# Moving the weight sums of a down-projection beside the up-projection, with its first left factors loaded and split early

## The chip, the cores and the metric

The kernel runs on one core of one Trainium2 chip. The metric is the device time of one execution in microseconds (us), as the median of three runs. The core has five engines that work at the same time, each through its own list of instructions in order: TensorE (PE, with its weight loads PEld), VectorE (DVE), ScalarE (ACT), GpSimd (POOL) and SyncE (SP). All DMA transfers of this kernel are issued by SP, in the order of its list.

## The reference, cut to what matters

One step of a decoder layer: a mixing block (an mLSTM beside a convolution module), cross-attention into 256 memory tokens, and a ConvFFN, for 2048 prompt tokens and 64 sample tokens. The change lies in the ConvFFN and at its entry.

```python
# D_MODEL = 1024, D_FF = 2816, SEQ = 2048, 8 sample rows of 8 tokens
hf = rmsnorm(x, w['norm_ffn'])
uf = hf @ w['f_wup']
fa, fg = uf[..., :D_FF], uf[..., D_FF:]
f_ext = jnp.concatenate([f_buf.astype(fa.dtype), fa], axis=1)
fa_c = causal_dwconv(f_ext, w['f_conv_w'], w['f_conv_b'])      # width 3
x = x + (jax.nn.gelu(fa_c) * fg) @ w['f_wdown']
...
y_prompt = rmsnorm(xp, norm_final)
```

All of it is float32, and the result must be that of float32 products.

## The kernel before, in words

**Products.** A float32 product is made of three matmuls: each operand is split into a high part (rounded to the matmul's type by a ScalarE cast) and a low part (the rest, a subtraction on VectorE or GpSimd), and `mm3` (L153) adds high x high, high x low and low x high. `split` (L295) makes the two parts. Large products are cut into two by two quarters and made of seven products instead of eight (`seven_products`, L1058): of each operand there are three quarters (B11, B21, B22) and four sums (T1 to T4), the "factors". `left_sums` (L1050) makes the four sums of one operand.

**Up-projection.** The prompt is taken in three blocks of 6, 5 and 5 row tiles of 128 tokens (`C_BLOCKS`); the last also has the sample tokens. `rows_in` loads and norms the rows of a block (six buffers `xt` in the pool `xw`), in two halves z; `block_input` transposes them and makes the seven right factors R. T1 and T4 are made on GpSimd. Then eleven steps p follow, each with two `load_pair` calls (for the value columns a and the gate columns g): raw weights come in, and seven split weights `wt` (a ring of ten tiles) go to `seven_products`. In block 0 the four sums of each weight pair are made and stored; blocks 1 and 2 load them. VectorE adds the products, convolves, and multiplies with the gate; the result's left factors for the down-projection go to DRAM (`l_d`).

**Down-projection.** For each of the seven products q (order B11, B21, T2, T3, T1, B22, T4) the eleven right factors are loaded and split (`right_factors_down`); for each of eight row tiles j a left factor `lr` (128 x 11 x 128) is loaded and split into `l`, and 33 matmuls of 512 columns follow. One (q, j) is called a unit here; there are 56, counted from 0. The row tiles `acc` (`x2_d`, the residual) are loaded beside the first two products: eight for B11, eight for B21. `weight_sums` runs beside units 1 to 11: it loads two 128-row slices of `f_wdown`, multiplies the sample rows with them (`psG`), makes the four sums on VectorE and GpSimd, and stores them (`ds`) for the products T2, T3, T1 and T4.

**What sets the order.** The code is written as a sequence; a scheduler then puts each engine's instructions in order, by the code's order and by when it reckons that operands and tiles are free, so that work can stand far from where the code has it. Tiles come from pools with a fixed number of buffers; a pool opened in the place of a closed one waits, tile by tile, for what lay in its memory. Pools with `side="right"` grow from the other end.

Of the kernel before, what the change touches and what calls it, by code (L numbers as in the profile page):

```python
# [19 lines left out]
P = 128  # L20
D = 1024
# [70 lines left out]
R_ORDER = 1, 2, 3, 0, 4, 5, 6  # L92
# [4 lines left out]
def trunk_kernel(ctx: ExitStack, tc: tile.TileContext, i: dict, o: list):  # L97
# [1341 lines left out]
    def rows_in(blk, junk=None):  # L1439

        t0, nt_, smp = blk
        hc = nt_ * P // 2
        halves = []
        for z in range(2):
            xts = []
            first, n = t0 * P + z * hc, hc + (HS if smp else 0)
            for c0 in range(0, n, P):
                nt = min(P, n - c0)
                t = xw.tile([P, D], F32, name="xt", tag="xt")
                c = c0  # L1450
                while c < c0 + nt:
                    if c < hc:
                        tid, r0 = divmod(first + c, P)
                        m = min(P - r0, c0 + nt - c, hc - c)
                    else:
                        tid, r0, m = NT, z * HS, HS
                    SY.dma_start(t[c - c0:c - c0 + m], x2_d[tid][r0:r0 + m])
                    c += m
                norm_x([(t, nt)], junk() if junk else fe_.tile([P, D], BF16, name="junk", tag="junk"), V)
                xts.append((t, nt))  # L1460
            halves.append(xts)
        return halves
# [158 lines left out]
    def factors():  # L1621
        return [wfp.tile([P, 2, KT // 2, 512], F32R, name=f"wf{q}", tag=f"wf{q}") for q in range(7)]
# [37 lines left out]
    ahead = rows_in(C_BLOCKS[0], junk_rows)  # L1660
# [5 lines left out]
    wtp = ctx.enter_context(tc.tile_pool(name="wtf", bufs=WT_BUFS, side="right", reuse_waits="tile"))  # L1666
    f2 = us.enter_context(tc.tile_pool(name="f2", bufs=2, side="right", reuse_waits="tile"))
# [10 lines left out]
    def block_input(blk, rows):  # L1678

        n = width(blk)  # L1680
        R = {}

        def btile():
            return fe_.tile([P, HM], F32, name="b", tag="b", bufs=KT)[:, :n]

        def feature(xts, k):
            pt = tps()
            c = 0
            for t, nt in xts:
# [9 lines left out]
        b11, t3 = [btile() for _ in half], [utile(n) for _ in half]  # L1699
        for q in R_ORDER:  # L1700
# [48 lines left out]
    def raw_tile():  # L1749
        return f2.tile([P, 2, 512], F32, name="raw", tag="raw", bufs=RAW_BUFS)  # L1750
# [54 lines left out]
    R_next = block_input(C_BLOCKS[0], ahead)  # L1805
    for bi, (t0, nt_, smp) in enumerate(C_BLOCKS):
# [6 lines left out]
        for p in range(FP):  # L1813
# [77 lines left out]
    lp = ctx.enter_context(tc.tile_pool(name="lp", bufs=2, side="right", reuse_waits="tile"))  # L1891
# [35 lines left out]

    sums_d = [[dram(f"ds{kh}_{k}", [P, 2, 512]) for k in range(FP)] for kh in range(2)]
# [4 lines left out]
    def weight_sums(k):  # L1933

        r = []
        for kh in range(2):
            t = xw.tile([P, 2, 512], F32, name="wr", tag="xt")
            SY.dma_start(t, wdn[(2 * k + kh) * P:(2 * k + kh + 1) * P, :].rearrange("p (c d) -> p c d", c=2))
            for c in range(2):
                mm(pts[c * S:(c + 1) * S], ysr[:, 2 * k + kh], t[:, c], k + kh == 0, k + kh == FP)  # L1940
            r.append(t)
        (b11, b12), (b21, b22) = [[t[:, c] for c in range(2)] for t in r]
        tt(b22, b22, b12, ALU.subtract)
        tt(b12, b12, b11, ALU.subtract, G)
# [22 lines left out]
    def left_factor(q, j):  # L1967
        raw = lp.tile([P, FP, P], F32, name="lr", tag="lr")
        r = 0
        for b, c, m in segments(j):  # L1970
            SY.dma_start(raw[:, :, r:r + m], l_d[b][q, :, :, c:c + m])
            r += m
        w = lp.tile([P, 2, FP, P], F32R, name="l", tag="l")
        split(w[:, 0], w[:, 1], raw)
        return w
# [9 lines left out]

    accs = [], []
    for qi, q in enumerate((B11, B21, T2, T3, T1, B22, T4)):
# [3 lines left out]
        for j in range(NJ):  # L1991
            l = left_factor(q, j)
            if qi < 2:
                accs[qi].append(acc_rows(qi, j))
            pt = dps()
            for k in range(FP):
                mm3(pt, (l[:, 0, k], l[:, 1, k]), (ws[k][:, 0], ws[k][:, 1]), k == 0, k == FP - 1)
            c = cs[j]
            x00, x01, x10, x11 = [accs[z][j][:, c_ * 512:(c_ + 1) * 512] if z <= qi else None
# [29 lines left out]
            if qi < 2 and 0 < qi * NJ + j <= FP:  # L2029
                weight_sums(qi * NJ + j - 1)  # L2030
# [3 lines left out]
        elif q == B21:  # L2034
# [37 lines left out]
```

## Time and profile before

| | us |
|---|---|
| runs | 2940.2, 2941.53, 2950.7 |
| median | 2941.53 |
| profiled execution | 2940.78 |
| its span | 2939.1 |
| TensorE busy | 2733.7 (93%) |
| VectorE busy | 2053.4 (70%) |
| ScalarE busy | 1395.5 (47%) |
| GpSimd busy | 1204.5 (41%) |

The span runs from the first to the last recorded instruction; 1.7 us lie around it. The ConvFFN takes the second half: the first matmul with R starts at 1466.5, the up-projection's last ends at 2450.8, the down-projection's last at 2931. A share over the whole span says little here, since the stages have different limits; the views by stage, below, are read with the time of each stage in mind. [...]

### The profile page before, as it was taken

Reading aid. Unit: us, or ns where it says so; the run is one execution under the profiler, and the core shown is the slowest. Engines: PE = TensorE matmul, PEld = TensorE weight load, DVE = VectorE, ACT = ScalarE, POOL = GpSimd, SP = SyncE. Lnnn points to the kernel's source line nnn. Section 1 sums busy time; section 2 is a strip of 40 time slices with the busy share of each in tenths; the row PEclk is TensorE's granted clock in tenths of the full one; section 3 lists DMA queues with packets and bytes.
Section 4 is the critical chain, followed back from the end, with each engine's and each line's share of the span. In section 5 each row is a group of like instructions: output and inputs, shape, how many; then the busy total and the mean of one; then the engine's idle time right before and its main releaser. Section 6 shows DMA issues by size and latency. Waiting matters only on the chain. (4 is left out here: it accounts for less than half of the span.)

```text
span 2939.1 us, 44186 instructions
## 1 busy us (share of the span) xinstructions
PE 2733.7 (93%) x15768; PEld 2409.4 (82%) x15768; DVE 2053.4 (70%) x3393; ACT 1395.5 (47%) x2777; POOL 1204.5 (41%) x1287
## 2 busy tenths in 40 slices
PE   7999999989799799899799999999999997899998
PEld 6889899966577778676589899899989996578887
DVE  4588898783224788755389999888898885354454
ACT  4576678871223665512364334644454452232233
POOL 1458565460220533534365444554464442113200
PEclk9999999998899999999899999999999998999999
DMA  7635433344557423757644555566656557994454
GB/s 184 196 123 181 125 91 120 90 155 140 180 171 238 159 69 100 241 177 248 215 157 164 178 182 167 173 205 197 198 173 187 174 178 225 307 290 137 138 167 131
DMA packets 428532, 509.37 MB, mean 173 GB/s; under 512 B 61613, under 2 KB 331667, under 8 KB 428304
## 3 DMA queue, kind: packets, MB, share of 16 engines
q1 hardware_dynamic: 428312, 506.55, 54.5%
q8 instruction: 124, 2.03, 0.3%
q14 instruction: 96, 0.79, 0.1%
HBM read 346.67 MB, written 160.15 MB: 172 GB/s over the span
## 5 line engine op out<-in xcount | busy, mean ns | idle before, releaser
L297 ACT CAST wt<-raw 128x512 fp32r<-128x512 f32 x542 | 325.6, 618 | 366.4 <-DVE raw L128 66.7
L128 DVE TENSOR_TENSOR wt<-raw,wt 128x512 fp32r<-128x512 f32 x374 | 337.5, 907 | 89.2 <-ACT wt L297 88.7
L128 POOL TENSOR_TENSOR wt<-raw,wt 128x512 fp32r<-128x512 f32 x168 | 251.5, 1498 | 192.3 <-ACT wt L297 171.6
L128 POOL TENSOR_TENSOR cside<-cside,cprod 128x512 f32<-128x512 f32 (+2 forms) x248 | 251.4, 1014 | 120.7 <-ACT cprod L120 82.3
L125 DVE SCALAR_TENSOR_TENSOR psG<-ue,vc,psG 128x512 f32<-128x512 f32 (+2 forms) x448 | 256.7, 573 | 22.8 <-ACT psG L120 15.2
L151 PE MATMUL psA<-R,wt 128*128 128x384 f32 (+2 forms) x1392 | 246.4, 328 | 6.0 <-DVE u L128 2.5
L151 PEld LDWEIGHTS psA<-R,wt 128*128 128x128 f32 x1392 | 229.3, 191 | 8.3 <-ACT wt L297 3.1
L297 ACT CAST l<-lr 128x1408 fp32r<-128x1408 f32 x56 | 77.1, 1376 | 284.2 <-PE psA L151 68.7
L120 ACT ACTIVATE cprod<-ue,vc 128x512 f32<-128x512 f32 (+2 forms) x248 | 146.8, 605 | 30.0 <-POOL cside L128 22.2
L151 PE MATMUL psA<-wf,l 128*128 128x512 f32 x516 | 133.0, 406 | 10.0 <-DVE u L128 5.8
L125 DVE SCALAR_TENSOR_TENSOR y<-fe,vc,y 128x640 f32<-128x640 f32 (+1 forms) x132 | 137.2, 1073 | 6.5 <-ACT y L120 6.5
L128 DVE TENSOR_TENSOR l<-lr,l 128x1408 fp32r<-128x1408 f32 x56 | 98.9, 1766 | 60.1 <-ACT l L297 57.5
L151 PE MATMUL psG<-R,wt 128*128 128x320 f32 (+2 forms) x696 | 128.7, 327 | 4.9 <-DVE fe L128 2.4
L151 PE MATMUL psE<-R,wt 128*128 128x352 f32 (+2 forms) x696 | 127.4, 326 | 5.7 <-DVE u L128 3.1
L151 PE MATMUL psD<-R,wt 128*128 128x320 f32 (+2 forms) x696 | 127.0, 326 | 5.5 <-DVE u L128 3.3
L151 PE MATMUL psC<-R,wt 128*128 128x384 f32 (+2 forms) x684 | 124.4, 328 | 7.8 <-DVE u L128 7.2
L144 POOL TENSOR_TENSOR r<-v,nhalf 128x1 f32<-128x1 f32 (+1 forms) x63 | 39.9, 634 | 222.6 <-DVE v L134 221.3
L151 PE MATMUL psF<-R,wt 128*128 128x352 f32 (+2 forms) x696 | 126.5, 325 | 3.2 <-DVE fe L128 2.5
L151 PEld LDWEIGHTS psA<-wf,l 128*128 128x128 f32 x516 | 97.6, 194 | 38.6 <-issue 13.2
L128 POOL TENSOR_TENSOR y<-y,u 128x384 f32<-128x384 f32 (+2 forms) x66 | 78.4, 1188 | 122.8 <-ACT wt L297 53.1
L151 PE MATMUL psB<-R,wt 128*128 128x384 f32 (+2 forms) x684 | 123.8, 326 | 1.3 <-DVE R L128 0.7
L151 PE MATMUL psD<-h,wt 128*128 128x256 f32 (+1 forms) x768 | 116.7, 297 | 7.5 <-DMA h<-h 4.8
(663 smaller groups left out, 6927.0 us busy)
## 6 DMA issues: line engine op xcount, KB each, us to landing
raw<-in_f_wup SPq DMA_DIRECT2D x88, 512.0 KB
raw<-sum SPq DMA_DIRECT2D x88, 512.0 KB
lr<-l SPq DMA_DIRECT2D x49, 704.0 KB
sum<-raw SPq DMA_DIRECT2D x44, 512.0 KB
xt<-x SPq DMA_DIRECT2D x42, 512.0 KB
xt<-in_x_prompt SPq DMA_DIRECT2D x32, 512.0 KB
x<-xt SPq DMA_DIRECT2D x32, 512.0 KB
h<-h SPq DMA_DIRECT2D x56, 256.0 KB
```

The source lines that it names most:

```text
L120: A.activation(out, in_, func, bias=bias, scale=scale)
L125: V.scalar_tensor_tensor(out=out, in0=in0, scalar=s, in1=in1, op0=op0, op1=op1)
L128: (eng or V).tensor_tensor(out=out, in0=a, in1=b, op=op)
L144: G.tensor_tensor(out=y, in0=v, in1=e.to_broadcast(sh), op=ALU.pow)
L151: T.matmul(out, lhsT, rhs, start=start, stop=stop)
L297: A.copy(hi, src)
```

## The change

- `weight_sums` is called in the up-projection, at the steps listed in `SUMS_AT` (block 1, p = 0 to 6, and block 2, p = 1 to 4); all four sums are on GpSimd, and it no longer multiplies the sample rows.
- `sample_rows` multiplies the sample rows with one 128-row slice of `f_wdown`, beside units 1 to 22; `f_wdown` is loaded for it once more (`ws`).
- The left factors are loaded two units ahead in the code (`left_raw`), the first two into buffers of `xw` shared with other tiles ("common"), with high priority; the first is split into three weight tiles (`left_first`). The buffers of `lr` lie in the pool `dp`, and `l` has two named tiles.
- The second eight `acc` tiles are loaded at the third product T2 in the code, not the second.
- `rows_in` takes one half z; of block 0, the second half is loaded and normed inside `block_input`, after the factors B11 and B21.
- The order in which pools and tiles are laid out changes: `wf` reversed, raw weights in a pool of their own, R in another order, the convolution's carries behind R.

```diff
-R_ORDER = 1, 2, 3, 0, 4, 5, 6
+SUMS_AT = [(1, p) for p in range(7)] + [(2, p) for p in range(1, 5)]
+ACC_AT = 0, 2
+R_ORDER = 1, 2, 3, 4, 0, 5, 6
...
-    def rows_in(blk, junk=None):
+    def rows_in(blk, z, junk=None):
...
-        return [wfp.tile([P, 2, KT // 2, 512], F32R, name=f"wf{q}", tag=f"wf{q}") for q in range(7)]
+        return [wfp.tile([P, 2, KT // 2, 512], F32R, name=f"wf{q}", tag=f"wf{q}") for q in range(6, -1, -1)][::-1]
...
-    ahead = rows_in(C_BLOCKS[0], junk_rows)
+    ahead = rows_in(C_BLOCKS[0], 0, junk_rows)
...
+    rawf = us.enter_context(tc.tile_pool(name="rawf", bufs=RAW_BUFS, side="right", reuse_waits="tile"))
...
-        xts, xts1 = rows
+        xts = rows[0]
...
+        xts1 = rows[1] if len(rows) > 1 else rows_in(blk, 1, lambda: junk)
         b12 = [btile() for _ in half]
...
+    def weight_sums(k):
+        r = []
+        for kh in range(2):
+            t = xw.tile([P, 2, 512], F32, name="wr", tag="xt")
+            SY.dma_start(t, wdn[(2 * k + kh) * P:(2 * k + kh + 1) * P, :].rearrange("p (c d) -> p c d", c=2))
+            r.append(t)
+        (b11, b12), (b21, b22) = [[t[:, c] for c in range(2)] for t in r]
+        tt(b22, b22, b12, ALU.subtract, G)
+        tt(b12, b12, b11, ALU.subtract, G)
+        tt(b11, b11, b22, ALU.add, G)
+        tt(b21, b21, b11, ALU.subtract, G)
+        for kh in range(2):
+            SY.dma_start(sums_d[kh][k], r[kh])
...
+            if (bi, p) in SUMS_AT:
+                weight_sums(SUMS_AT.index((bi, p)))
...
-            for c in range(2):
-                mm(pts[c * S:(c + 1) * S], ysr[:, 2 * k + kh], t[:, c], k + kh == 0, k + kh == FP)
...
+    def sample_rows(f):
+        t = xw.tile([P, 2, 512], F32, name="ws", tag="xt")
+        SY.dma_start(t, wdn[f * P:(f + 1) * P, :].rearrange("p (c d) -> p c d", c=2))
+        for c in range(2):
+            mm(pts[c * S:(c + 1) * S], ysr[:, f], t[:, c], f == 0, f == FT - 1)
...
+    def left_first(raws):
+        out = []
+        for k0, raw in raws:
+            for c in range(0, raw.shape[1], 4):
+                n = min(4, raw.shape[1] - c)
+                w = next(w_turn)().rearrange("p z (k t) -> p z k t", k=4)
+                split(w[:, 0, :n], w[:, 1, :n], raw[:, c:c + n])
+                out += [(w[:, 0, k], w[:, 1, k]) for k in range(n)]
+        return out
...
+    with tc.high_priority():
+        ahead = [left_raw(B11, j, True) for j in range(2)]
+    first = left_first(ahead.pop(0))
...
-            l = left_factor(q, j)
-            if qi < 2:
-                accs[qi].append(acc_rows(qi, j))
+            l = left_factor(ahead.pop(0)) if qi + j else first
+            n_ = qi * NJ + j + 2
+            if n_ < len(ORDER) * NJ:
+                ahead.append(left_raw(ORDER[n_ // NJ], n_ % NJ))
+            if qi in ACC_AT:
+                accs[ACC_AT.index(qi)].append(acc_rows(ACC_AT.index(qi), j))
...
-            if qi < 2 and 0 < qi * NJ + j <= FP:
-                weight_sums(qi * NJ + j - 1)
+            if 0 < qi * NJ + j <= FT:
+                sample_rows(qi * NJ + j - 1)
```

ScalarE at the entry of block 0, before: `junk` is the square sum of a row tile's norm, `xt<-xt,r` its scaling, `wt` a weight's cast, `b` the first transposed quarter of the rows and `R` its cast.

```order
L297 CAST l<-a 128x512 x5
L122 ACTIVATE junk,ss<-xt 128x1024
L120 ACTIVATE xt<-xt,r 128x1024 x2
L297 CAST wt<-raw 128x512 x9
L122 ACTIVATE junk,ss<-xt 128x1024
L120 ACTIVATE xt<-xt,r 128x1024
L122 ACTIVATE junk,ss<-xt 128x1024
L120 ACTIVATE b<-psB,vc_432 128x384
L120 ACTIVATE b<-psC,vc_432 128x384
L297 CAST R_15356<-b 128x384
```

And the same engine and place in the change (lines are three further on):

```order
L300 CAST l<-a 128x512 x5
L123 ACTIVATE xt<-xt,r 128x1024
L300 CAST wt<-raw 128x512 x2
L123 ACTIVATE b<-psB,vc_432 128x384
L123 ACTIVATE b<-psC,vc_432 128x384
L125 ACTIVATE junk,ss<-xt 128x1024
L300 CAST R_15327<-b 128x384 x2
L123 ACTIVATE b<-psB,vc_432 128x384
L123 ACTIVATE b<-psC,vc_432 128x384
L123 ACTIVATE xt<-xt,r 128x1024
L300 CAST wt<-raw 128x512 x5
```

The first `b` stood behind nine casts and the norms of the second half's rows; now it stands behind two casts, and the rest comes after it.

SP's queue at the entry of the down-projection, before, behind the last store of block 2: `lr` is a left factor, `acc<-x_n` rows of tile n of the residual, `wr` weights, `ysr` the sample rows.

```order
L1971 DMA lr<-l_15305 128x11x128
L1923 DMA acc<-x_0_186 128x1024
L2024 DMA ysr<-ys 128x1408
L2027 DMA accs<-x_16_202 64x512 x2
L1971 DMA lr<-l_15305 128x11x128
L1923 DMA acc<-x_1_187 128x1024
L1923 DMA acc<-x_2_188 128x1024
L1923 DMA acc<-x_6_192 128x1024
L1938 DMA wr<-in_f_wdown 128x1024
L1923 DMA acc<-x_7_193 128x1024
```

And in the change, where the first `lr` here is that of unit 2 (those of units 0 and 1 stand in block 2), and `ws` is a slice for the sample rows:

```order
L1985 DMA lr<-l_15274 128x11x128
L1944 DMA acc<-x_0_186 128x1024
L2064 DMA ysr<-ys 128x1408
L2067 DMA accs<-x_16_202 64x512 x2
L1985 DMA lr<-l_15275 128x11x128
L1944 DMA acc<-x_1_187 128x1024
L1944 DMA acc<-x_2_188 128x1024
L1955 DMA ws<-in_f_wdown 128x1024
L1944 DMA acc<-x_6_192 128x1024
L1955 DMA ws<-in_f_wdown 128x1024
L1944 DMA acc<-x_7_193 128x1024
L1955 DMA ws<-in_f_wdown 128x1024
```

The left factors are two units further on at the same place in the queue; the `acc` loads, those of the second eight too, stand where they stood, with `ws` loads between.

GpSimd at the entry of block 1, before: `b` and `R` make the factor T1, `u` the factor T4, `r` belongs to the norm of block 2's rows.

```order
L128 TENSOR_TENSOR b<-b 128x320
L144 TENSOR_TENSOR r<-v,nhalf 128x1
L231 MEMSET ss 128x4
L128 TENSOR_TENSOR R_18926<-b,R_18926 128x320
L128 TENSOR_TENSOR b<-b 128x320
L144 TENSOR_TENSOR r<-v,nhalf 128x1
L128 TENSOR_TENSOR u<-R_18922,u 128x320
L128 TENSOR_TENSOR u<-u,R_18922 128x320
```

And in the change, where `wr` is one of the weight sums:

```order
L131 TENSOR_TENSOR b<-b 128x320
L131 TENSOR_TENSOR wr<-wr 128x512
L131 TENSOR_TENSOR R_18949<-b,R_18949 128x320
L131 TENSOR_TENSOR b<-b 128x320
L131 TENSOR_TENSOR wr<-wr 128x512
L131 TENSOR_TENSOR u<-R_18946,u 128x320
L131 TENSOR_TENSOR b<-b 128x320
L131 TENSOR_TENSOR R_18949<-b,R_18949 128x320
L131 TENSOR_TENSOR wr<-wr 128x512
```

The norms of block 2's rows have moved out of this place, and weight sums stand between the instructions that make T1 and T4.

## Rows read from the trace of the kernel before

**Rows 1.** Busy time by stage: start:end, length, each engine (instructions), clock, DMA.

```profile
1450.00:1490.00 40.00, 20.05 (x89) 15.97 (x89) 26.92 (x44) 28.20 (x51) 16.74 (x21) 0.70 0.62 204
1500.00:1840.00 340.00, 316.99 (x1765) 310.95 (x1763) 332.70 (x410) 139.90 (x228) 174.17 (x156) 0.98 0.53 174
1880.00:2120.00 240.00, 239.91 (x1635) 239.54 (x1635) 215.54 (x322) 119.37 (x197) 120.87 (x120) 1.00 0.64 199
2451.00:2480.00 29.00, 14.28 (x48) 9.59 (x46) 9.47 (x15) 4.34 (x5) 3.19 (x3) 0.71 0.98 300
2480.00:2520.00 40.00, 35.58 (x139) 25.04 (x138) 12.00 (x12) 5.77 (x6) 8.35 (x6) 0.91 1.02 286
2700.00:2900.00 200.00, 200.00 (x884) 165.62 (x883) 103.54 (x113) 64.44 (x78) 38.90 (x27) 1.00 0.53 150
```

**Rows 2.** TensorE's waits from 1440 to 1500: total us, times, longest.

```profile
PE psB L148 <- ACT b L120: 17.4, 2, 16.2
```

**Rows 3.** TensorE's timeline in the down-projection: start, us, instruction, count.

```profile
2450.85 0.38 PE L148 MATMUL psB<-ident,cy_s 128*16 128x128 f32 x2
...
2467.17 9.01 PE L151 MATMUL psA<-wt,l 128*128 128x512 f32 x28 [0.44 <-DVE l L128]
...
2479.11 6.66 PE L151 MATMUL psB<-wt,l 128*128 128x512 f32 x28
...
2606.74 1.08 PE L151 MATMUL psG<-wr,ysr 128*64 128x512 f32 x4
2607.75 1.89 PE L151 MATMUL psE<-wt,l 128*128 128x512 f32 x7
2609.48 2.88 PE L151 MATMUL psF<-w,l 128*128 128x512 f32 x12
...
2684.28 2.20 PE L151 MATMUL psC<-wt,l 128*128 128x512 f32 x9
```

**Rows 4.** TensorE's waits from 2451 to 2640.

```profile
PE psA L151 <- ACT l L297: 17.8, 2, 14.3
PE psB L151 <- ACT wt L297: 5.3, 1, 5.3
```

**Rows 5.** ScalarE's casts of the left factors of units 0 and 6.

```profile
2464.10 1.36 ACT L297 CAST l<-lr 128x1408 fp32r<-128x1408 f32 x1 [12.07 <-DMA lr<-l]
...
2527.42 1.38 ACT L297 CAST l<-lr 128x1408 fp32r<-128x1408 f32 x1 [3.58 <-DMA lr<-l]
```

**Rows 6.** DMA issues by size.

```profile
lr<-l SPq DMA_DIRECT2D x49, 704.0 KB
...
wr<-in_f_wdown SPq DMA_DIRECT2D x22, 512.0 KB
ds<-wr SPq DMA_DIRECT2D x22, 512.0 KB
...
acc<-x SPq DMA_DIRECT2D x10, 512.0 KB
```

**Rows 7.** ScalarE's timeline at the entry of block 0.

```profile
1448.88 0.62 ACT L297 CAST wt<-raw 128x512 fp32r<-128x512 f32 x1 [4.37 <-PE psA L151]
1455.90 3.74 ACT L297 CAST wt<-raw 128x512 fp32r<-128x512 f32 x7 [6.40 <-DVE raw L128]
...
1464.65 0.56 ACT L120 ACTIVATE b<-psB,vc 128x384 f32<-128x384 f32 x1
```

**Rows 8.** Sums on GpSimd, weights in blocks 1 and 2, the last T4 sum.

```profile
L128 POOL TENSOR_TENSOR wr<-wr 128x512 f32<-128x512 f32 x22 | 32.9, 1500 | 123.7 <-DVE wr L128 117.1 <-issue 5.7 <-DMA ds<-wr 0.9
...
1915.15 0.62 ACT L297 CAST wt<-raw 128x512 fp32r<-128x512 f32 x1 [1.15 <-PE psA L151]
1916.90 0.62 ACT L297 CAST wt<-raw 128x512 fp32r<-128x512 f32 x1 [1.13 <-PE psA L151]
...
1875.89 1.36 POOL L128 TENSOR_TENSOR u<-u,R 128x320 f32<-128x320 f32 x1
...
L128 DVE TENSOR_TENSOR wt<-raw,wt x210: 671/685/1803, 1871.7 to 2430.1; 128x512 fp32r<-128x512 f32 x105
...
L128 DVE TENSOR_TENSOR wt<-raw,wt 128x512 fp32r<-128x512 f32 x99 | 91.4, 924 | 11.4 <-ACT wt L297 11.4
```

More of the change, by code (lines that the diff above doesn't have):

```diff
@@ L1437, in out_rows @@
             SY.dma_start(x2_d[t], xt)
-    def rows_in(blk, junk=None):
+    def rows_in(blk, z, junk=None):
         t0, nt_, smp = blk
         hc = nt_ * P // 2
[L1443 to L1462, printed above, removed]
+        xts = []
+        first, n = t0 * P + z * hc, hc + (HS if smp else 0)
+        for c0 in range(0, n, P):
+            nt = min(P, n - c0)
+            t = xw.tile([P, D], F32, name="xt", tag="xt")
+            c = c0
+            while c < c0 + nt:
+                if c < hc:
+                    tid, r0 = divmod(first + c, P)
+                    m = min(P - r0, c0 + nt - c, hc - c)
+                else:
+                    tid, r0, m = NT, z * HS, HS
+                SY.dma_start(t[c - c0:c - c0 + m], x2_d[tid][r0:r0 + m])
+                c += m
+            norm_x([(t, nt)], junk() if junk else fe_.tile([P, D], BF16, name="junk", tag="junk"), V)
+            xts.append((t, nt))
+        return xts
     def own_tiles(pp):
@@ L1749, in raw_tile @@
     def raw_tile():
-        return f2.tile([P, 2, 512], F32, name="raw", tag="raw", bufs=RAW_BUFS)
+        return rawf.tile([P, 2, 512], F32, name="raw", tag="raw")
     sum_d = {}
@@ L1804, in trunk_kernel @@
     wa_next = load_pair(0, True)
-    R_next = block_input(C_BLOCKS[0], ahead)
+    R_next = block_input(C_BLOCKS[0], [ahead])
+    carry = fe_.tile([P, FT, 2], F32, name="carry")
+    G.memset(carry, 0.0)
+    fst = fe_.tile([P, FT, 2 * NB], F32, name="fst")
+    cy_s = fe_.tile([P, FT, 2 * NB], F32, name="cy_s")
+    sums_d = [[dram(f"ds{kh}_{k}", [P, 2, 512]) for k in range(FP)] for kh in range(2)]
+    def weight_sums(k):
[11 more added lines that the diff above has]
+            SY.dma_start(sums_d[kh][k], r[kh])
     for bi, (t0, nt_, smp) in enumerate(C_BLOCKS):
@@ L1876, in trunk_kernel @@
                     SY.dma_start(ys_d[:, f0 + m].rearrange("p (z t) -> p z t", z=2), ys[m][:, :, hc:])
+            if (bi, p) in SUMS_AT:
+                weight_sums(SUMS_AT.index((bi, p)))
             if bi + 1 < len(C_BLOCKS):
                 if p == FP - 3:
-                    rows_next = rows_in(C_BLOCKS[bi + 1])
+                    rows_next = [rows_in(C_BLOCKS[bi + 1], z) for z in range(2)]
                 if p == FP - 1:
@@ L1887, in trunk_kernel @@
     us.close()
-    lp = ctx.enter_context(tc.tile_pool(name="lp", bufs=2, side="right", reuse_waits="tile"))
+    lp = ctx.enter_context(tc.tile_pool(name="lp", bufs=1, side="right", reuse_waits="tile"))
     dp = ctx.enter_context(tc.tile_pool(name="dp", bufs=1, reuse_waits="tile"))
@@ L1925, in acc_rows @@
         return t
-    sums_d = [[dram(f"ds{kh}_{k}", [P, 2, 512]) for k in range(FP)] for kh in range(2)]
     SUMS = {T2: (0, 0), T1: (0, 1), T4: (1, 0), T3: (1, 1)}
@@ L1965, in right_factors_down, with left_raw, left_factor @@
         return out
[L1967 to L1975, printed above, removed]
+    def left_raw(q, j, common=False):
+        if common:
+            raws = [(0, xw.tile([P, KT, P], F32, name="lr", tag="xt")), (KT, xw.tile([P, FP - KT, P], F32, name="lr", tag="xt"))]
+        else:
+            raws = [(0, dp.tile([P, FP, P], F32, name="lr", tag="lr", bufs=2))]
+        for k0, raw in raws:
+            r = 0
+            for b, c, m in segments(j):
+                SY.dma_start(raw[:, :, r:r + m], l_d[b][q, :, k0:k0 + raw.shape[1], c:c + m])
+                r += m
+        return raws
+    def left_factor(raws):
+        z = next(l_side)
+        w = lp.tile([P, 2, FP, P], F32R, name=f"l{z}", tag=f"l{z}")
+        for k0, raw in raws:
+            ks = slice(k0, k0 + raw.shape[1])
+            split(w[:, 0, ks], w[:, 1, ks], raw)
+        return [(w[:, 0, k], w[:, 1, k]) for k in range(FP)]
+    def left_first(raws):
+        out = []
+        for k0, raw in raws:
+            for c in range(0, raw.shape[1], 4):
[4 more added lines that the diff above has]
+        return out
     def out_norm(t, nt, dsts):
@@ L1984, in out_rows_norm @@
         out_norm(accs[z][j], P, [(y_prompt[0, t0:t0 + m], r, m) for t0, m, r in token_rows(z, j)])
+    l_side = cycle((1, 0))
+    l_room = [lp.tile([P, 2, FP, P], F32R, name=f"l{z}", tag=f"l{z}") for z in range(2)]
     accs = [], []
-    for qi, q in enumerate((B11, B21, T2, T3, T1, B22, T4)):
+    ORDER = B11, B21, T2, T3, T1, B22, T4
+    with tc.high_priority():
+        ahead = [left_raw(B11, j, True) for j in range(2)]
+    first = left_first(ahead.pop(0))
+    for qi, q in enumerate(ORDER):
         ws = right_factors_down(q)
@@ L2033, in trunk_kernel @@
             SY.dma_start(nf, i["norm_final"].partition_broadcast(P))
-        elif q == B21:
+        elif q == T2:
             tt(accs_s, accs_s, pts, ALU.add)
```

22 lines of the change are left out of this document (3 added, 19 removed).

## The prediction

> **What bounds the kernel now.** I read the busy times by stage first, then who waited for whom on TensorE in the stages that are not full, then these stretches in order of time, and last the DMA sizes. The change touches everything from 1440 us on; what stands before keeps its order. Four stretches behave differently. (1) The entry of the first up-projection block, 1450 to 1490: TensorE is busy 20 of 40 us at a granted clock of 0.70, VectorE 26.9, ScalarE 28.2 [rows 1]; one wait for ScalarE's `b` takes 16.2 us [rows 2]. (2) The rest of block 0, 1500 to 1840: VectorE is busy 332.7 of 340 us, so it sets the pace, and a us that VectorE begins earlier is a us at the end. (3) Blocks 1 and 2: TensorE is busy 239.9 of 240 us, VectorE 215.5 (90%), GpSimd 120.9 (50%) [rows 1]. TensorE cannot gain here, only lose. (4) The down-projection from 2451: 56 units (a product q and a row tile j), each 7.48 us when nothing is in the way (ten of them from 2609.48 to 2684.28) [rows 3]. From 2700 to 2900 TensorE is full. Before that it is not: 14.3 of 29 us up to 2480, 35.6 of 40 after it, with the DMA engines at shares of 0.98 and 1.02 [rows 1]. Waits there: 17.8 us for the left factor `l`, 5.3 us for the right factor `wt` [rows 4]. 23 units (172.0 us) and the 22 sample row groups (44 matmuls; a group of two takes 1.0 us, from 2606.74 to 2607.75, so 21 to 22 us) need 194 us; before takes 2684.3 - 2451.2 = 233 us [rows 3]. So 39 us are lost at the front of this stage, in waits and at the low level of the clock: after the 14.3 us wait, 28 matmuls took 9.01 us, where 6.66 is usual [rows 3]. This is where there is something to win.
>
> **Down-projection: first factors early, sums gone.** In the changed order the left factors of units 0 and 1 are loaded during block 2, and the first is split before block 2 ends, so the 14.3 us wait goes. What is late next is the left factor of unit 2 and all behind it, because the queue behind it is still full: 16 row tiles `acc` of 512 KB go out between the `lr` loads, and the second eight, though asked for later in the code, still stand before the left factor of unit 5. So I count bytes. Before, from the cast of `lr` 0 (2464.10) to that of `lr` 6 (2527.42) [rows 5] the queue moved acc 8192, ysr 704, accs 256, nf 512, six lr 4224, three wr 1536 and six sum stores 3072, together 18,496 KB (sizes of the first, the weights and the stores [rows 6], the others by their shapes) in 63.3 us: 292 KB/us. Change: the up-projection ends as before (2451), `lr` 2 is the first load behind the last `ls` store and lands when `lr` 0 landed, 2464.1. Then, at 292 KB/us: lr 3 behind 2176 KB, 2471.6; lr 4 behind 4544 (seven of 512, 256, 704), 2487.2; lr 5 behind 7104, 2511.5; lr 6 behind 2240, 2519.2; lr 7 behind 3008 (the weights of B21 among them), 2529.5. TensorE: units 0 to 3 run from about 2452.5 to 2485.5 with three sample groups; unit 4 waits for lr 4 and its 1.4 us cast, 2488.6 to 2496.1; four sample groups to 2500; unit 5 starts at 2512.9 (a wait of 13 us in place of the one removed), takes 2.7 us more at the low clock, and ends at 2523.1; unit 6 2530.6; unit 7 2538.4. From there a unit and a sample group need 8.5 us, and about 1.6 MB move in that time, under the rate. Fifteen units and 15 groups later unit 23 starts at 2538.4 + 112.2 + 15 = 2665.6, against 2684.3: **-18.7 us**. The 5.3 us wait for `wt` at unit 8 is gone in this, since no stores stand before those weights any more. The bounds: -39 if the loads never hold TensorE, and 0 if the queue holds it as long as before. Reading the 11.3 MB of down weights twice costs only queue time, counted above. The sample rows now take 22 groups of two matmuls for eleven of four, at about 0.1 us more a group: 1 us, put at nothing. TensorE's last unit and the output norm behind it stay as they are.
>
> **Entry of block 0: -5.5 us.** Before, ScalarE's first `b` stands behind nine weight casts, the last seven of which wait 6.40 us for VectorE's sums, and behind the norms of two rows of the second half; it runs at 1464.65, though TensorE's last attention product and the transposes beside it are done at 1449 (they release the cast of 1448.88) [rows 7]. In the change it stands behind two casts and can run at 1449.5. The second half's rows are normed after it, so those instructions are moved, not removed. VectorE's low part of R now stands behind its weight sums, which end at 1455.9 [rows 7], so the first full matmuls can come some 10 us earlier. But ScalarE's work up to 1490 is the same 28.2 us; what is won is its idle 6.40 us [rows 7], into which 5.6 us of `b`, R and one norm move. After that casts, which before came first, come between the R's, and loads of block 1's rows stand in SP's queue before the third weight load. I take 5.5. Bounds: 0, and 13.1 us, VectorE's whole idle time there (40 - 26.9) [rows 1].
>
> **Weight sums beside the up-projection: +3 us.** Eleven times four sums go to GpSimd, where one took 1.50 us [rows 8]: 44 x 1.5 = 66 us. The order does not spread them over eleven steps p, as the code's table reads: 28 stand in the entry and the first three steps p of block 1 (some 66 us of TensorE) and 16 in one and a half steps of block 2. GpSimd at 50% and 28 x 1.5 = 42 us make 75 us of work in 66: up to 9 us late. Cover: the ten `wt` tiles. In block 1 ScalarE casts a weight as soon as TensorE frees a tile, every 1.76 us [rows 8], so a weight is ready some nine products, 15 us, ahead; 9 us of lateness are hidden. If that cover were gone they would be paid. Not covered is the entry of block 1: GpSimd makes the T1 and T4 factors there, now with nine sums (13 us) between, and the last T4 sum ended at 1877.25 [rows 8], as TensorE was waiting for it. GpSimd's idle time takes up half, and TensorE is given 22 matmuls of the next pair (3 us) to run meanwhile. I take 3 us. Bounds: 0 and +36 (below). It cannot gain, since TensorE is full there.
>
> Contention: a VectorE low part takes 0.685 us (median), at most 1.803 [rows 8], and the long ones lie beside GpSimd instructions. At the mean of the stage (0.92, from 91.4 us for 99) GpSimd's doubled load costs VectorE about 2.5 us a step of 22, just its idle tenth. [...]
>
> Other edits (layout of the pools, order of R, `wf` reversed) move no work; they decide which tile waits for which memory. R in the new order puts the `lr` buffers over a factor last used five products before the end of block 2, so they don't add a wait. Cost 0, bounds -3 to +5, the size of waits for R at an entry.
>
> **Sum.** -18.7 - 5.5 + 3 = -21. The profiled execution took 2940.8 us (span 2939.1 and 1.7 around it), the median of the runs is 0.7 above: 2941.5 - 21 = **2920.5 us**.
>
> **Rivals.** (a) The queue stays the bound: the row tiles hold the left factors of units 4 to 7 longer (274 KB/us, the rate up to `lr` 4, or `ws` loads waiting for a free tile with `lr` behind them), the down-projection gains 8, the entry 5: 2932. For it: shares of 1.02; against: 3 MB of stores are gone from that stretch. (b) GpSimd and SP's queue hold blocks 1 and 2: a store of sums waits in SP's queue for GpSimd, and weight loads stand behind it; five raw tiles for a pair that needs four give them little lead. At 3 us for each of the eleven, +33 on top of the rest: 2953, slower than before. For it: GpSimd is over-full in that stretch, VectorE at 90%; against: the 15 us lead. It decides as soon as TensorE's busy share in block 1 falls below 95%. (c) The loads never hold TensorE: -39 in place of -18.7, 2900. (d) The early factors do nothing, because the split or its tiles come late: 2935.
>
> **Chances.** Forecast 0.55 (own range 2909 to 2929), (a) 0.20, (b) 0.12, (c) 0.10, (d) 0.03. About 0.5% (14.7 us) is what can be told from no change, so faster means under 2926.8: most of the forecast (0.47), (c), a little of (a): 0.60. Slower, over 2956.2, is the worse half of (b): 0.07. The rest, 0.33, is the same. Range 2903 to 2942: it leaves out most of (b) and of (c).
>
> **What will show it.** Right: the wait before the first matmul of the down-projection is under 3 us, there is a wait of about 13 us for `l` near unit 5, unit 23 starts some 215 us after the up-projection's last matmul (233 before), block 1 stays over 97% busy on TensorE, `b` runs at about 1450 and the up-projection ends 2 to 3 us earlier than before. Wrong: TensorE idle in the first 70 us of blocks 1 and 2 with GpSimd full (then b), or no wait at unit 5 (then c).

## The result, and the profile after

The changed kernel takes 2961.43 us (median of four runs, 2956.3 to 2962.2) against 2940.86 us for the kernel before on the same chip: a ratio of 1.0063, 95% interval 1.0047 to 1.0079. It is slower by 0.63%, where 0.7% faster was forecast. The end of a stage moves by up to 13 us from run to run with what lies before it (attention's last product ends anywhere from 1443 to 1456 us in the profiles below), so stages are compared by their lengths, from one profiled execution of each kernel: "up" runs from attention's last product to the last matmul with R, "down" from there to the last matmul of all.

| | up, us | down, us | both |
|---|---|---|---|
| before | 1002.0 | 480.5 | 1482.5 |
| changed | 1033.1 (+31.1) | 469.9 (-10.6) | 1503.0 (+20.5) |

Busy time by stage in the changed kernel, with the columns of [rows 1] (the clock is TensorE's granted clock, 1.00 when full); the two rows of 20 us lie in block 1's first steps:

```profile
1450.00:1490.00 40.00, 24.77 (x91) 18.30 (x89) 30.19 (x47) 29.98 (x55) 21.55 (x24) 0.70 0.64 206
1500.00:1840.00 340.00, 314.75 (x1763) 307.64 (x1762) 333.07 (x412) 141.36 (x231) 170.14 (x155) 0.98 0.53 174
1880.00:2120.00 240.00, 227.70 (x1513) 224.65 (x1512) 215.03 (x304) 123.35 (x205) 150.19 (x145) 0.99 0.73 238
1900.00:1920.00 20.00, 18.77 (x127) 18.27 (x125) 19.96 (x24) 8.20 (x14) 15.81 (x15) 1.00 0.93 314
1920.00:1940.00 20.00, 16.73 (x104) 16.76 (x105) 19.92 (x26) 6.30 (x10) 19.36 (x16) 0.91 0.98 340
...
2482.00:2520.00 38.00, 34.77 (x146) 24.90 (x144) 16.12 (x23) 9.98 (x14) 3.25 (x3) 1.00 0.95 293
2520.00:2560.00 40.00, 25.78 (x94) 17.50 (x95) 7.77 (x9) 6.18 (x8) 0.00 (x0) 0.79 0.98 284
...
2700.00:2900.00 200.00, 199.77 (x881) 164.18 (x880) 106.00 (x120) 69.12 (x85) 40.21 (x27) 1.00 0.56 162
```

And the 95 us in which the first 28 sums run, in the same kernel:

```profile
1852.00:1947.00 95.00, 82.49 (x502) 78.11 (x503) 87.70 (x105) 40.24 (x75) 87.55 (x73) 0.95 0.76 264
```

The same three stretches of the kernel before:

```profile
1900.00:1920.00 20.00, 19.91 (x136) 19.65 (x135) 19.28 (x29) 9.75 (x16) 10.39 (x11) 1.00 0.62 190
1920.00:1940.00 20.00, 20.00 (x139) 20.00 (x138) 19.22 (x28) 10.47 (x18) 11.80 (x12) 1.00 0.66 208
...
1852.00:1947.00 95.00, 90.95 (x579) 86.15 (x580) 85.47 (x135) 59.02 (x106) 57.86 (x62) 0.98 0.61 182
```

**Blocks 1 and 2.** TensorE falls from 239.9 [rows 1] to 227.7 of 240 us, 94.9% busy. Read the counts beside VectorE's busy time: in the 95 us it is busy a little longer (87.70 us, 85.47 before), but has done 105 instructions where it did 135, and in 40 of them it has no time left (39.88 us). Its instructions have become longer. The groups of VectorE from 1880 to 2440 (busy us, mean ns of one | idle before) show which; in the kernel before:

```profile
L128 DVE TENSOR_TENSOR wt<-raw,wt 128x512 fp32r<-128x512 f32 x207 | 178.5, 863 | 26.1 <-ACT wt L297 25.7
L125 DVE SCALAR_TENSOR_TENSOR y<-fe,vc,y 128x640 f32<-128x640 f32 x84 | 79.8, 981 | 1.3 <-ACT y L120 1.3
...
L128 DVE TENSOR_TENSOR u<-u,psA 128x320 f32<-128x320 f32 (+1 forms) x50 | 24.5, 497 | 6.7 <-PE psA L151 3.3 <-ACT y L120 3.1
```

and in the changed kernel, with GpSimd's sums `wr` behind them:

```profile
L131 DVE TENSOR_TENSOR wt<-raw,wt 128x512 fp32r<-128x512 f32 x198 | 186.8, 951 | 21.5 <-ACT wt L300 21.0
L128 DVE SCALAR_TENSOR_TENSOR y<-fe,vc,y 128x640 f32<-128x640 f32 x80 | 83.7, 1077 | 2.4 <-ACT y L123 2.3
...
L131 DVE TENSOR_TENSOR u<-u,psA 128x320 f32<-128x320 f32 (+1 forms) x50 | 24.4, 497 | 10.5 <-PE psA L154 8.6 <-ACT y L123 1.5
...
L131 POOL TENSOR_TENSOR wr<-wr 128x512 f32<-128x512 f32 x37 | 57.3, 1554 | 0.1
```

A weight's low part `wt` takes 88 ns more on average, a convolution step `y` 96 ns; 198 x 0.088 + 80 x 0.096 is 25 us. A sum on GpSimd takes 1.55 us, near the 1.50 of [rows 8]. The sum `u`, which reads one operand from PSUM, takes 497 ns in both. TensorE feels it through VectorE: the longest of its waits from 1832 to 1960 in the changed kernel are all for VectorE, for the sums `u` and for the factors R at the entry:

```profile
PE psA L154 <- DVE u L131: 3.7, 1, 3.7
PE psA L154 <- DVE R L131: 1.9, 1, 1.9
PE psC L154 <- DVE R L131: 1.9, 1, 1.9
PE psF L154 <- DVE u L131: 1.5, 1, 1.5
```

**Entry of block 0.** ScalarE's first `b`, which ran at 1464.65 [rows 7], runs as soon as TensorE has transposed its rows:

```profile
1448.48 0.58 ACT L123 ACTIVATE b<-psB,vc 128x384 f32<-128x384 f32 x1 [2.27 <-PE psB L151]
```

The 16.2 us wait for it [rows 2] is gone, and TensorE's first matmul with R comes 15 us earlier than before. The next ones wait for VectorE:

```profile
1451.03 0.44 PE L154 MATMUL psA<-R,wt 128*128 128x384 f32 x1 [0.89 <-ACT R L300]
...
1456.33 1.33 PE L154 MATMUL psA<-R,wt 128*128 128x384 f32 x3 [3.86 <-DVE R L131]
```

Counted from attention's last product, the 672nd matmul with R ends at 162.7 us before and at 160.8 us after: VectorE is 98% busy from 1500 to 1840 in both kernels, and of the 15 us some 2 are left. Kernels 4 and 10 of the experiments, which have the old entry, stand at 162.5 and 160.8 there, so that even these 2 us are within what such times differ by.

**Down-projection.** The wait of 14.3 us ahead of its first matmul [rows 4] is gone. TensorE's timeline from there, as in [rows 3]:

```profile
2481.68 5.05 PE L154 MATMUL psA<-wt 128*128 128x512 f32 x21
...
2515.60 1.08 PE L154 MATMUL psG<-ws,ysr 128*64 128x512 f32 x4
2518.36 0.73 PE L154 MATMUL psD<-wt,l 128*128 128x512 f32 x2 [1.68 <-ACT l L300]
...
2527.28 2.80 PE L154 MATMUL psG<-ws,ysr 128*64 128x512 f32 x12
2538.27 1.98 PE L154 MATMUL psG<-ws,ysr 128*64 128x512 f32 x4 [8.20 <-DMA ws<-in_f_wdown]
2545.82 1.22 PE L154 MATMUL psE<-wt,l 128*128 128x512 f32 x2 [5.57 <-ACT l L300]
2547.47 6.84 PE L154 MATMUL psE<-wt,l 128*128 128x512 f32 x19 [0.44 <-DVE l L131]
```

Unit 5 (`psE`) starts at 2545.8, 64.3 us after the up-projection; unit 4 (`psD`) at 36.9. SP's queue shows what stands between their left factors:

```profile
2502.44 0.56 SPq L1985 DMA_DIRECT2D lr<-l  x1
2504.99 4.25 SPq L1944 DMA_DIRECT2D acc<-x  x1
...
2517.96 6.51 SPq L1944 DMA_DIRECT2D acc<-x  x5
...
2526.24 5.63 SPq L1944 DMA_DIRECT2D acc<-x  x4
2533.57 3.56 SPq L1985 DMA_DIRECT2D lr<-l  x2
```

Between the loads of `lr` at 2502.44 and 2533.57, those of units 4 and 5, the queue issues 14 loads of `acc`, nine of them for the second half, which is not needed before the fourth product.

### The profile page after: what moved, and what is told of

Read it like the earlier page. It is cut to its first block, busy times and chain, and to the rows that moved or that the text cites. A ratio compares the mean times of both kernels' runs of the same rounds, so it can differ in the third digit from the quotient of the medians.

```text
span 2959.2 us, 44220 instructions
## 1 busy us (share of the span) xinstructions
PE 2745.1 (93%) x15768; PEld 2410.5 (81%) x15768; DVE 2070.8 (70%) x3374; ACT 1394.3 (47%) x2780; POOL 1234.3 (42%) x1309
## 5 line engine op out<-in xcount | busy, mean ns | idle before, releaser
L131 DVE TENSOR_TENSOR wt<-raw,wt 128x512 fp32r<-128x512 f32 x374 | 354.8, 956 | 81.7 <-ACT wt L300 81.0
L300 ACT CAST l<-lr 128x1408 fp32r<-128x1408 f32 (+2 forms) x56 | 75.6, 1352 | 276.4 <-PE psA L154 68.4
L128 DVE SCALAR_TENSOR_TENSOR y<-fe,vc,y 128x640 f32<-128x640 f32 (+1 forms) x132 | 144.6, 1128 | 7.5 <-ACT y L123 7.4
L131 POOL TENSOR_TENSOR acc<-acc,c 128x512 f32<-128x512 f32 x24 | 42.6, 1791 | 246.4 <-DVE c L131 240.3
L131 DVE TENSOR_TENSOR l<-lr,l 128x1408 fp32r<-128x1408 f32 (+2 forms) x56 | 95.7, 1711 | 63.5 <-ACT l L300 61.3
L154 PEld LDWEIGHTS psG<-R,wt 128*128 128x128 f32 x696 | 117.1, 195 | 11.9 <-DVE R L131 4.4
```

What stands on the lines that cost most here:

```text
L128: V.scalar_tensor_tensor(out=out, in0=in0, scalar=s, in1=in1, op0=op0, op1=op1)
L131: (eng or V).tensor_tensor(out=out, in0=a, in1=b, op=op)
L154: T.matmul(out, lhsT, rhs, start=start, stop=stop)
L300: A.copy(hi, src)
```

## The experiments

Ratios are to the kernel before, run on the same chip, with their 95% intervals; up and down as above, from each one's profile.

| | median us | ratio | up | down |
|---|---|---|---|---|
| 1 sums back | 2939.0 | 0.9990 (0.9977 to 1.0003) | 1003.8 | 475.3 |
| 2 no arithmetic | 2937.0 | 0.9983 (0.9966 to 0.9999) | 1006.6 | 468.0 |
| 3 sums spread | 2941.7 | 1.0006 (0.9991 to 1.0020) | 1016.0 | 470.8 |
| 4 before, sums moved | 2962.5 | 1.0078 (1.0061 to 1.0095) | 1030.1 | 473.5 |
| 5 `acc` held back | 2940.3 | 1.0003 (0.9988 to 1.0017) | 1029.6 | 449.9 |
| 6 memsets for sums | 2938.2 | 0.9992 (0.9977 to 1.0006) | 1007.5 | 471.4 |
| 7 combined | 2911.4 | 0.9902 (0.9881 to 0.9922) | 1003.3 | 450.8 |
| 8 spread, `acc` held back | 2919.3 | 0.9931 (0.9910 to 0.9951) | 1009.9 | 450.6 |
| 9 before, halves only | 2936.5 | 1.0004 (0.9991 to 1.0018) | 1003.9 | 478.7 |
| 10 before, sums moved, `acc` held back | 2958.7 | 1.0082 (1.0062 to 1.0102) | 1029.5 | 466.2 |

**1. Is it the sums at all?** The sums go back into the down-projection, with the rest of the change kept.

```diff
-            if (bi, p) in SUMS_AT:
-                weight_sums(SUMS_AT.index((bi, p)))
...
-            if 0 < qi * NJ + j <= FT:
-                sample_rows(qi * NJ + j - 1)
+            if qi < 2 and 0 < qi * NJ + j <= FP:
+                weight_sums(qi * NJ + j - 1)
```

> The changed kernel with only the weight sums (and the sample rows with them) put back beside the first two products of the down-projection, half of them on VectorE, as the kernel before has them. In the changed kernel the up-projection's last matmul ends 30.7 us later than before (2481.5 against 2450.8) and the down-projection behind it is 10.6 us shorter. Theory A (GpSimd's 44 sums crowd the entry and the first steps of blocks 1 and 2) and theory B (the sums' 88 transfers of 512 KB fill SP's queue and the DMA engines there): the up-projection ends at 2451 again, the early left factors keep part of the gain, total 2930 to 2938. Theory C (the relaid pools, the raw tiles' own pool, the order of R or the halves cost the 31 us): it still ends at about 2481 and the total stays at 2960 or above.

Up is back at 1003.8 us. Theory C falls: pools, order of R, `rawf` and halves together cost no more than 2 us. The total, 2939.0, is just over the 2930 to 2938 expected, because the early left factors win only 5 us in the down-projection.

**2. Arithmetic or transfers?**

```diff
-        tt(b22, b22, b12, ALU.subtract, G)
-        tt(b12, b12, b11, ALU.subtract, G)
-        tt(b11, b11, b22, ALU.add, G)
-        tt(b21, b21, b11, ALU.subtract, G)
```

> The changed kernel without the 44 subtractions and additions of the weight sums: their loads and stores stay, the products T1 to T4 of the down-projection then use unsummed weights. Theory A (GpSimd's arithmetic, through lateness or through VectorE's slower instructions): the up-projection ends 25 us or more earlier, at 2450 to 2456, total about 2933. Theory B (the transfers): it still ends at 2475 or later, total about 2957. A mixture shows as a time between, and its share is read from it.

Up falls by 26.5 us (1033.1 to 1006.6) with all 88 transfers still there; these are left with 1006.6 - 1002.0 = 4.6 us at most. (The last matmul with R ends at 2462.6 in this profile, later than expected, since attention's last product ended 7.6 us later; the lengths are what is compared.) Theory B falls, except for these few us.

**3. Crowding or number?**

```diff
             t = xw.tile([P, 2, 512], F32, name="wr", tag="xt")
+            G.tensor_copy(t[:, 0, :2], step)
...
-                weight_sums(SUMS_AT.index((bi, p)))
+                weight_sums(SUMS_AT.index((bi, p)), carry[:, f0])
```

> The changed kernel with each set of four sums tied to its own step p: two columns of the carry of step p are copied into each wr tile by GpSimd before its load, so that a set can't be loaded before that step. The order then has four sums in each of seven steps of block 1 and of four of block 2 instead of 28 in the entry and three steps. If the crowding and the sums ahead of the T1 and T4 factors cost the time, the up-projection ends at 2451 to 2461 and the total is 2930 to 2940. If the 44 sums cost by their sheer number, wherever they stand (VectorE slowed by them, or the transfers), it stays at 2475 or later, total about 2957.

Up takes 1016.0, between the two: some 17 of the 31 us are crowding, 14 remain (8 in kernel 8, which is the same up to the down-projection, so the split is good to some 6 us). The total lies 2 us over the first range. VectorE's groups from 1880 to 2440 in this run:

```profile
L131 DVE TENSOR_TENSOR wt<-raw,wt 128x512 fp32r<-128x512 f32 x202 | 177.8, 886 | 25.7 <-ACT wt L300 25.4
L128 DVE SCALAR_TENSOR_TENSOR y<-fe,vc,y 128x640 f32<-128x640 f32 x84 | 96.7, 1182 | 1.0 <-ACT y L123 1.0
```

The excess over the kernel before, 202 x 0.023 + 84 x 0.201 = 22 us, is about as large as in the changed kernel. Spreading does little to the excess as a whole (low parts take 886 ns, 951 in the changed kernel, but steps `y` 1182, 1077 there); it lets more of it fall into VectorE's idle tenth (VectorE is busy 510.5 of these 560 us, 500.4 in the changed kernel).

**4. The sums alone, in the kernel before.** Its `weight_sums` is replaced by that of the changed kernel, called at `SUMS_AT`, and `sample_rows` by its loop; nothing else.

```diff
+            if (bi, p) in SUMS_AT:
+                weight_sums(SUMS_AT.index((bi, p)))
...
-            if qi < 2 and 0 < qi * NJ + j <= FP:
-                weight_sums(qi * NJ + j - 1)
+            if 0 < qi * NJ + j <= FT:
+                sample_rows(qi * NJ + j - 1)
```

> The kernel before with only the sums moved beside blocks 1 and 2 on GpSimd, as in the changed kernel; left factors, pools and halves as before. Theories A and B: the up-projection ends some 30 us later, the down-projection gains a few us for the sums and stores that are gone from it, total 2962 to 2972. Theory C: the up-projection ends at 2451 to 2455, total 2930 to 2940.

28.1 us up, 7.0 us won down, and the total as expected: the move of the sums is the whole loss, with the old pools too.

**5. What holds unit 5.**

```diff
         t = dp.tile([P, D], F32, name="acc", tag=f"acc{z}_{j}")
+        if z or j > 2:
+            G.tensor_copy(t[:, :2], (accs[0][j] if z else cs[j - 3])[:, :2])
```

> The changed kernel with the row tiles acc held back: two columns of an earlier result are copied into a row tile by GpSimd before its load (of row j - 3 of the first product for the first eight from j = 3 on, of the second product's row j for the second eight), so the queue can't take them all at the front. In the changed kernel unit 4 of the down-projection starts 36.9 us after the up-projection and unit 5 64.3 us after it, where 8.7 are usual; 14 loads of acc stand between their left factors. Theory Q (those loads are what unit 5 waits for): units 4 to 6 follow at 8.7 us, the down-projection takes about 449 us (469.9), total about 2941. Rival: the same bytes come later and hold the units from 8 on, or the sample rows' ws loads hold it anyway: 460 or more, total 2952 or above.

All of TensorE's waits in the first 200 us of the down-projection are now these:

```profile
PE psD L154 <- DVE l L131: 0.7, 1, 0.7
PE psA L154 <- DVE w L131: 0.7, 2, 0.4
PE psG L154 <- DMA ysr<-ys: 0.4, 1, 0.4
```

Unit 5 starts at 45.3 us, not 64.3, and the stage takes 449.9, the total 2940.3. Theory Q holds: the `acc` loads were the wait, and given later they hold nothing.

**6. Late, or lengthened?**

```diff
+NSET = 3
...
-        tt(b22, b22, b12, ALU.subtract, G)
...
+        for x in (b22, b12, b11, b21):
+            for _ in range(NSET):
+                G.memset(x, 0.0)
```

> The changed kernel with each of the 44 sums replaced by three memsets of the same 512 columns on GpSimd (one of 516 columns took 0.53 us in the kernel before, so 1.6 us for a sum of 1.55); the loads and stores stay, the products T1 to T4 of the down-projection then use weights without their sums. GpSimd is as late as with the sums, but reads no SBUF operand for them. Theory V (VectorE's instructions are made longer beside GpSimd's sums): VectorE's low part of a weight in blocks 1 and 2 falls from 951 ns to about 870, its y from 1077 to about 990, the up-projection from its 1680th recorded R matmul takes under 682 us (701 changed, 673 without the arithmetic), total about 2941. Theory L (GpSimd comes late with its own T1 and T4 factors, low parts and products): 695 us or more, total 2955 or above.

Groups of VectorE and GpSimd from 1880 to 2440:

```profile
L132 DVE TENSOR_TENSOR wt<-raw,wt 128x512 fp32r<-128x512 f32 x205 | 178.4, 876 | 30.8 <-ACT wt L301 30.4
L129 DVE SCALAR_TENSOR_TENSOR y<-fe,vc,y 128x640 f32<-128x640 f32 x84 | 82.1, 1006 | 2.1 <-ACT y L124 1.9
...
L1821 POOL MEMSET wr<- 128x512 f32 x112 | 54.4, 523 | 1.9 <-DMA wr<-in_f_wdown 1.9
```

GpSimd is held for 54.4 us in the same places (57.3 with the sums), VectorE's means are back near those of the kernel before, at 876 and 1006 ns (ScalarE's weight casts take 0.62 us with either), and up is 1007.5, with a total of 2938.2. From the 1680th matmul with R on, the up-projection takes 655.6 us here, 680.9 in the changed kernel and 654.2 without the arithmetic. (The expectation's 701 and 673 come from a count in which some matmuls stand twice; its bounds are some 20 us too high by that, and 655.6 is on theory V's side of them either way.) Theory V holds: of 31 us, lateness of GpSimd and the transfers together make 5.5, and 25.6 come with sums in place of memsets, beside which VectorE's instructions are longer. One pair of moments shows it. In the changed kernel, VectorE, then GpSimd, then TensorE around 1917 us:

```profile
1916.46 3.07 DVE L131 TENSOR_TENSOR wt<-raw,wt 128x512 fp32r<-128x512 f32 x2
...
1921.34 0.47 DVE L131 TENSOR_TENSOR u<-u,psG 128x320 f32<-128x320 f32 x1
```

```profile
1917.23 1.75 POOL L131 TENSOR_TENSOR wr<-wr 128x512 f32<-128x512 f32 x1
...
1920.83 1.72 POOL L131 TENSOR_TENSOR wr<-wr 128x512 f32<-128x512 f32 x1
```

```profile
1917.62 1.92 PE L154 MATMUL psA<-R,wt 128*128 128x320 f32 x12
1923.27 2.73 PE L154 MATMUL psA<-R,wt 128*128 128x320 f32 x12 [3.73 <-DVE u L131]
```

and with memsets, VectorE and then GpSimd:

```profile
1917.98 0.68 DVE L132 TENSOR_TENSOR wt<-raw,wt 128x512 fp32r<-128x512 f32 x1
```

```profile
1917.64 0.98 POOL L1821 MEMSET wr<- 128x512 f32 x2
```

Beside a sum, and a product of GpSimd ahead of it, two low parts take 3.07 us, beside memsets one takes 0.68; the PSUM sum `u` runs through a GpSimd sum in 0.47. Then TensorE, which has waited 3.73 us for `u`, takes 2.73 us for the twelve matmuls that took 1.92 before: behind the wait the granted clock falls to 0.50, from 1924.5 to 1927.5 (1.00 from 1917 to 1920).

**7. A version that beats both.** The sums are back in the down-projection and spread over three products, none of which needs them, and `acc` is held back.

```diff
-    ORDER = B11, B21, T2, T3, T1, B22, T4
+    ORDER = B11, B21, B22, T2, T3, T1, T4
...
+            if j % 2 and (qi * NJ + j) // 2 < FP:
+                weight_sums((qi * NJ + j) // 2)
```

> A version meant to beat both: the changed kernel with the sums back beside the down-projection (half on VectorE), one set in every second unit over the first three products, which are now B11, B21, B22 (none of them needs a sum; the norm of the first half's rows moves to T1), and the row tiles acc held back as in the run before, the second eight to the fourth product. The sums back alone gave 2939.0 with 475.3 us in the down-projection. If the queue at its front is what is left, it takes 450 to 457 us here, total 2914 to 2921; if the 22 MB of sums and raw weights hold TensorE wherever they are put, 470 or more, total 2934 or above.

2911.4 us, a ratio of 0.9902 to the kernel before and so some 50 us below the changed one. Waits of TensorE in the first 200 us of its down-projection:

```profile
PE psG L154 <- DMA wr<-in_f_wdown: 3.1, 1, 3.1
PE psA L154 <- DVE w L131: 0.7, 2, 0.3
PE psG L154 <- DMA ysr<-ys: 0.2, 1, 0.2
```

The sums cost nothing to speak of there once the queue in front is spread out: 450.8 us, against 449.9 and 450.6 in runs 5 and 8 without them.

**8. Spread sums and `acc` held back**: the edits of 3 and 5 together.

> The changed kernel with the sums spread over the steps p (2941.7 alone, the down-projection 470.9 us) and the row tiles acc held back. Theory Q: the down-projection takes about 450 us, total about 2921. Rival (the loads hold later units instead): 460 or more, total 2932 or above.

As expected by theory Q. It is 8 us slower than 7, and up is 6.6 us longer: what the spread sums still cost beside the up-projection.

**9. The entry alone**: in the kernel before, `rows_in` takes one half, and block 0's second half is normed in `block_input`.

```diff
-    ahead = rows_in(C_BLOCKS[0], junk_rows)
+    ahead = rows_in(C_BLOCKS[0], 0, junk_rows)
...
-        xts, xts1 = rows
+        xts = rows[0]
...
+        xts1 = rows[1] if len(rows) > 1 else rows_in(blk, 1, lambda: junk)
```

> The kernel before with only the rows of block 0 brought in by halves (second half normed after the first half's factors). The prediction gave this entry 5.5 us. In the changed kernel the first R matmul came 15 us earlier, but after 672 recorded R matmuls both kernels stood 152 us behind attention's last product. If VectorE, busy throughout block 0, takes the gain back, it is so here too and the total is 2937 to 2943; if the entry is worth its 5.5 us when nothing else changes, the 672nd comes at about 147 us and the total is about 2935.

The first R matmul comes at 3.1 us (17.6 before), the 672nd ends at 160.4 (162.7), the 1344th at 289.3 (291.6). (The expectation's 152 and 147 come from the same count as above; 5.5 us earlier would be 157.2.) So the lead shrinks to some 2 us within block 0, and it doesn't last: at block 0's last matmul this kernel is 3.9 us ahead, two steps into block 1 0.7, one step into block 2 it is 1.9 us behind, and so it stays. The ratio is 1.0004: no gain.

**10. Are the early left factors worth anything?** The edit of 5 on kernel 4, with the second eight `acc` asked for at T2.

> The kernel before with the sums moved beside blocks 1 and 2 (2962.5 alone, the down-projection 473.5 us) and the row tiles acc held back, but with the left factors loaded and split as before. It tells what the early left factors are worth once the queue is free: with them and acc held back the down-projection took 449.9 us. If the wait of 14 us before its first product is then all that they remove: 464 us, total about 2953. If without the acc loads that wait shrinks by itself, 455 us or less, total 2945 or less; if the pacing is worth little without them, 470 or more, total about 2960.

The down-projection takes 466.2 us, near the first case's 464, and this is all that TensorE waits for in its first 200 us:

```profile
PE psA L152 <- ACT l L298: 14.2, 1, 14.2
PE psA L152 <- DVE l L129: 0.4, 1, 0.4
```

The median (2958.7) is 5 us over the expected 2953 and its ratio is not told apart from that of 4, so this run rests on its profile. By the profiles the early factors, with the pools laid out for them, are worth 473.5 - 469.9 = 3.6 us with the queue full, and 466.2 - 449.9 = 16.3 with `acc` held back.

## Why the prediction was wrong

**The failed step is the price of the weight sums, +3 us, where the up-projection lost 31 (28 to 29 of them go with the sums in runs 1 and 4).** Its own parts fared differently. The count from the order (28 sums in the entry and three steps, 16 in block 2) was right. The cover for GpSimd's lateness held: with GpSimd as busy, but with memsets (54.4 us of them in run 6, 57.3 of sums), the stage loses 5.5 us, transfers included. What failed is the sentence on contention, that GpSimd's doubled load "costs VectorE about 2.5 us a step of 22, just its idle tenth". It took the stage's mean of 0.92 us, in which more than half of the instructions have nothing beside them, as the price beside a sum. The timelines give that price: of the 205 low parts that start from 1865 to 2450 in the changed kernel, 98 have no GpSimd arithmetic beside them and take 0.68 us, as in the kernel before; 19 that lie at least half beside a sum take 1.47 on average. In run 6, 11 that have memsets beside them, and no arithmetic, take 0.68. In all, VectorE's 25 us of excess come to 0.44 us for each us of the 57.3 that GpSimd summed; 28 sums of 1.55 us then cost VectorE 19 us, an estimate from these figures, within the 95 us in which they run (1852 to 1947), a tenth of which it had to spare. In the fullest 40 us nothing was left of that, and TensorE ran dry behind it (16.73 of 20 us busy from 1920).

The runs show the price by what stands beside: a low part took 1.47 us beside sums and 0.68 beside memsets, as alone; the sum `u`, with one operand in PSUM, took 0.49 us where at least half of it lay beside a weight sum (19 in the changed kernel, 1840 to 2450) and 0.50 with no GpSimd arithmetic beside it. The prediction had the longest low part, 1.803 us, and saw that the long ones lie beside GpSimd instructions, and then went by the median and the mean; the median said only that more than half of the instructions had no GpSimd arithmetic beside them.

**Rival (b) came true in size, not in mechanism.** It gave +33 for blocks 1 and 2 (31 measured) and its sign, TensorE below 95% in block 1, was met (94.9%). But it put the time down to stores and weight loads in SP's queue; these are the 4.6 us of run 2, and with GpSimd as long at work ahead of each store, in run 6, no more than 5.5. That its size fits is luck.

**Entry: -5.5 forecast, 2 to 4 us seen within block 0, none at the end of the stage.** The steps on ScalarE came as worked out (`b` at 1448.48), but ScalarE was not what the stage waits for. The text itself had VectorE setting the pace of block 0, and the gain would have had to be counted there: from 1450 to 1490 VectorE is busy 30.2 us, 26.9 before, and the changed kernel is 2.3 us ahead at the 1680th matmul with R and 4.1 at block 0's last. Run 9 shows that such a lead is gone after the entries of the next two blocks; what takes it there is not shown.

**Down-projection: -18.7 forecast, -10.6 measured, the mechanism right.** The wait at the front went and came back at unit 5, as worked out, for the row tiles. Two sizes were off. Unit 6 starts 75.4 us after the up-projection, where the text has 72.1 (2523.1 - 2451). TensorE's wait ahead of unit 5 is 13.8 us, near the 13 forecast, but in two parts, 8.2 for `ws` and 5.6 for `l`, with a sample group between them that takes 1.98 us at a granted clock of 0.50 (1.08 at 1.00), and the unit behind it takes 11.1 us, not 10.2 (its granted clock is 0.60 up to 2554). And a unit with a sample group takes 8.7 us, not 8.5, so that unit 23 comes at 222.2, not 214.6; these 7.6 us are nearly all of the difference (8.1). Rival (c) was the queue without the row tiles; run 5 made it so, and 20 us came at once.

**Sum.** +31.1 (the entry is in it) - 10.6 is +20.5 in the profiles; 0.63% of 2940.9 is 18.5 in the runs.

**What stays open.** The 25.6 us are tied to GpSimd's sums, as against memsets, as a whole. How they divide, between VectorE's overrun, the raw tiles that it frees late (ScalarE's casts wait 10.2 us for `raw<-sum` from 1880 to 2000, never before) and matmuls at a lower granted clock (0.50 from 1924.5 to 1927.5), was not taken apart. Where they are lost is on record. Set against the kernel before at the same matmul with R, the changed kernel is 4.1 us ahead at block 0's end, then loses 14.6 us in the first three steps of block 1, which have the 28 sums, 7.2 in the next two, nothing in the other six, 12.1 in the first three steps of block 2, which have the other 16, and 1.4 in the rest. With memsets the five figures are 5.0, 1.7, 0, 2.6 and 0.7. The 7.2 us fall after the sums: there ScalarE waits 7.1 us for the `r` of block 2's norms on GpSimd and 4.6 for `raw<-sum` (1948 to 2005), so part of the price is paid late.

## What to carry to other kernels

Before work goes to an engine that is half idle, ask what it does to the full one beside it: price a GpSimd instruction by what VectorE's instructions take beside one (here a low part 1.47 us beside a sum, 0.68 beside memsets), not by a median or a stage's mean, and put it where VectorE has room (here the down-projection, VectorE 52% busy from 2700 to 2900). Count a gain at a stage's entry by the engine that sets the stage's pace: here 15 us of an earlier first matmul came to nothing. A load into a buffer of its own goes into the queue as early as the scheduler likes; a copy of two columns from a result of the right time holds it back (run 5: the down-projection takes 449.9 us in place of 469.9). The early factors, worth 3.6 us behind the full queue, were worth 16.3 once that was done.

## What the runs showed of the hardware

GpSimd's time as such was nearly free to VectorE: 112 recorded memsets of 0.52 us in the same places, beside a VectorE that was 87% busy, left its low parts at 876 ns (863 before), while 37 recorded sums of as much time in all (57.3 us, 54.4 of memsets) raised them to 951. A low part at least half beside a sum took 1.47 us on average and up to 1.79, in place of 0.68.
